# The last 256 tokens of a final RMSNorm transposed on TensorE before they are scaled, and the output stored in fewer, larger pieces

## The chip, the core and the metric

One Trainium2 chip, of which the kernel uses one core. The time is that of the device, in microseconds (us) from the launch to the end, for one execution; a median of several executions is given. The core has five engines with a queue each, worked in order: TensorE (PE, matmuls; PEld is its loading of the stationary operand), VectorE (DVE), ScalarE (ACT), GpSimd (POOL) and SyncE (SP, which here only issues DMA transfers). ACT and POOL can issue transfers too. Matmuls write to PSUM; the other tiles lie in SBUF. Both have 128 partitions.

## The reference

One layer of a hybrid mixer over 1024 tokens of 1024 features, in float32, and a final RMSNorm:

```python
shift, scale, gate = jnp.split(c_act @ mod_w[l] + mod_b[l], 3, axis=-1)
h = rmsnorm(x, norm_g[l]) * (1.0 + scale[:, None, :]) + shift[:, None, :]
cv, cg, cs, lx, ls = jnp.split(h @ w_in[l], [...], axis=-1)
v = causal_depthwise_conv(cv * jax.nn.sigmoid(cg), dw_w[l], dw_b[l])
v = jax.nn.silu(layernorm(v, cln_g[l], cln_b[l])) @ pw2_w[l] + pw2_b[l]
y_conv = v * jax.nn.silu(cs)
...
y_lru = linear_scan(a, mult * (i * xs)) * jax.nn.silu(ls)
y = jnp.concatenate([y_conv, y_lru], axis=-1) @ w_out[l]
x = x + (1.0 + gate[:, None, :]) * y
return rmsnorm(x, final_g)
```

The change touches the last three lines: `x` is what the kernel calls `fin`, and `rmsnorm` divides each token by the root of its mean square over the features and multiplies each feature by `final_g`.

## The kernel before

**Layout.** Everything is kept turned: features on partitions, tokens along the free axis. A tile `fin{m}` holds features 128m to 128m+127 of all 1024 tokens. A mean over features is therefore a sum over partitions and over eight tiles. The output leaves in the same layout, one row of the DRAM tensor a feature, and the host transposes it.

**Products.** A float32 product is three matmuls in a faster format: each operand is split into a high and a low part (`wh`, `wl`, `bh`, `bl` in `pair_products` and `tail_mm`), and low times low is left out. For pairs of output tiles, `pair_products` (L593) forms seven block products for eight: "1", "z", "2", "3", "4", "y" and "s", in the order of a string. "1", "2", "3" and "4" add up in one PSUM buffer `x` and in between ACT copies it to SBUF (`fout` after "1", `eout` after "2" and "3"): the next product into `x` has to wait for that copy. `OUT7` holds the strings for the product with w_out, for its three pairs; tile 6 comes before them and tile 7 (`OUT_Z`) is formed as a plain product.

**The scheduler.** `S` is a `Plan`, a list scheduler that runs when the program is built. Each operation has an engine, an estimated cost and a priority (the first argument, lower is earlier), reads and writes. Plan simulates the engines with these costs and so fixes the order of each engine's queue. The constants near the top (`ZP`, `NPZ`, `APART`, `SQP0`, `QGATES`, ...) are priorities and gates by which that order was adjusted; the order is no longer changed on the chip.

**The end.** The output is finished in three stretches of tokens, `END = ((0, 512), (512, 768), (768, 1024))`. `last_tiles` forms tile 7 of a stretch with 24 matmuls (L658; `out` in the profile). `gated` multiplies by 1 + gate and adds x (DVE, L360). `squares` squares each tile on ACT and sums the squares: tile 6 begins the sum `finss`, the others are added to it by DVE, and tile 7's are kept apart in `finsqz`, so that they need not be added.

`norm(n, a, e)` then makes the final norm of a stretch, through `rstd`: PE multiplies `finss` and `finsqz` by a column of ones (L680), which leaves the sum of squares of 128 tokens as one column of PSUM; ACT takes the root (`sd`), DVE the reciprocal (`rs`, L695). Since tokens lie along the free axis of `fin`, one more pair of matmuls spreads it: `rs` broadcast as the stationary operand times the identity (`spread`, L686) gives a PSUM tile `finbc` that holds 1/rms of every token on all partitions:

```python
pe.matmul(ps()[:, o + b * P:o + b * P + P],
          rs()[:, b:b + 1].to_broadcast([P, P]), ident, start=True, stop=True)
```

For the last stretch PE spreads it twice, into `finbc` for DVE and into `idle` for ACT, and executes seven matmuls without use (`warm_mm`, L676) in between. DVE makes `o = fin * final_g * finbc` for five or six of the eight tiles (L360), and POOL the others (L368), from a copy `bc` that ACT makes of the spread (L341) and from tiles `fin` that ACT has multiplied by `final_g`. Each of the eight tiles of a stretch is stored by itself (`store`, L392): eight stores of 256 KB for the first 512 tokens (2 KB rows), eight of 128 KB for each of the other stretches (1 KB rows); SP issues 18 of them and ACT six.

## Time and profile before

| | |
|---|---|
| time, median of 3 executions | 736.63 us (736.36 to 737.24) |
| time of the profiled execution | 736.94 us |
| its span, from the first instruction to the last | 735.2 us |
| granted TensorE clock | 0.999 |
| instructions | 8918 |

The profile is of one execution. Its span is 1.7 us shorter than that execution's time, which has the launch and the end around it. A row of a timeline gives the start, the length, the engine, the line of the kernel, the operation, its output and inputs (buffer numbers left out), their shapes as partitions x elements, the number of instructions and, in brackets, how long the engine was idle before and what ended that. PEq, DVEq, ACTq and SPq are the engines' sequencers, which issue transfers and wait for semaphores. In the table of windows each engine has its busy time and its number of instructions. An fp32 matmul leaves two records and a matmul in the faster format one.

### The profile page before, as it was taken

The page shows a single profiled execution, that of the slowest core. Times are in us where ns is not written, and L with a number is a line of the kernel's source. Part 1 is how long each engine was busy: PE and PEld are TensorE (multiplying, and loading weights), DVE is VectorE, ACT ScalarE, POOL GpSimd, SP SyncE. Part 2 cuts the span into 40 slices and gives each one's busy share as a digit, 9 for nine tenths or more (in the row PEclk, how much of TensorE's full clock was granted, in tenths as well). Part 3 has the DMA queues.
Part 4 walks back from the last instruction along what each step waited for, and adds up shares of the span by engine and source line. Part 5 has one row for each costly group of instructions (what it writes and reads, how often), then busy time and mean ns, then how long its engine had stood idle before and what let it go on. Part 6 is the DMA issues. An engine that isn't in the chain of part 4 may idle for free.

```text
span 735.2 us, 8918 instructions
## 1 busy us (share of the span) xinstructions
PE 727.7 (99%) x3312; PEld 605.8 (82%) x3312; DVE 623.7 (85%) x844; ACT 448.0 (61%) x563; POOL 110.0 (15%) x113
## 2 busy tenths in 40 slices
PE   9999999999999999999999999999999999999996
PEld 8888888888888888888888888878888888888886
DVE  7999999889979996887698999658799667999745
ACT  7650688556699968857859777334754323665432
POOL 0022001222312332321201110620000000000003
PEclk9999999999999999999999999999999999999999
DMA  9960045696979999789644453425233530522306
GB/s 341 407 221 29 0 131 120 142 211 149 237 177 227 211 211 225 160 178 213 129 113 100 114 104 109 163 97 201 86 114 111 177 114 1 204 94 103 115 1 229
DMA packets 37484, 111.59 MB, mean 152 GB/s; under 512 B 4160, under 2 KB 12864, under 8 KB 37440
## 3 DMA queue, kind: packets, MB, share of 16 engines
q1 hardware_dynamic: 24048, 75.97, 29.0%
q0 software_dynamic: 12528, 34.26, 26.3%
q10 hardware_dynamic: 864, 0.79, 0.3%
q8 instruction: 26, 0.43, 0.2%
q14 instruction: 18, 0.15, 0.1%
HBM read 64.16 MB, written 12.58 MB: 104 GB/s over the span
## 4 chain that ended last, share of the span: by engine, by line
PE 98%; DVE 1%; ACT 0%; DVEq 0%; issue 0%
PE ps L485 65%; PE xpw L607 6%; PE first L761 5%; PE xout L607 4%; PE ypw L607 3%; PE gate L1167 3%; PE out L658 2%; PE yout L607 2%; PE zpw L607 1%; PE zout L607 1%; DVE o L360 1%; PE late L761 1%; PE token_stats L718 1%; PE c_row L722 0%; PE token_stats L890 0%; PE vout L607 0%
## 5 line engine op out<-in xcount | busy, mean ns | idle before, releaser
L485 PE MATMUL ps<-ul,whi 128*128 128x512 f32 x576 | 177.4, 389 | 0.0
L485 PE MATMUL ps<-uh,whi 128*128 128x512 f32 x576 | 177.4, 389 | 0.0
L485 PE MATMUL ps<-uh,wlo 128*128 128x512 f32 x576 | 177.3, 389 | 0.0
L485 PEld LDWEIGHTS ps<-ul,whi 128*128 128x128 f32 x576 | 108.1, 188 | 22.5
L485 PEld LDWEIGHTS ps<-uh,wlo 128*128 128x128 f32 x576 | 108.1, 188 | 22.5
L485 PEld LDWEIGHTS ps<-uh,whi 128*128 128x128 f32 x576 | 108.1, 188 | 22.3
L341 ACT CAST whi<-raw 128x1024 fp32r<-128x1024 f32 x46 | 48.2, 1050 | 65.6 <-PE ps L485 52.4
L373 POOL DMA_DIRECT2D es<-cq x45 | 39.2, 872 | 230.1 <-ACT cq L349 209.7
L368 DVE TENSOR_TENSOR wlo<-raw,whi 128x1024 fp32r<-128x1024 f32 x42 | 52.3, 1244 | 14.0 <-ACT whi L341 14.0
L349 ACT ACT_TABLE_LOAD x45 | 57.7, 1283 | 1.5 <-PEq L1476 0.7
L360 DVE SCALAR_TENSOR_TENSOR cacc<-v,V,cacc 128x511 f32<-128x511 f32 (+14 forms) x75 | 55.8, 744 | 0.5
L360 DVE SCALAR_TENSOR_TENSOR caccs<-c,wsum,caccs 128x511 f32<-128x511 f32 (+6 forms) x70 | 52.1, 745 | 0.9
L360 DVE SCALAR_TENSOR_TENSOR caccs<-v,V,caccs 128x511 f32<-128x511 f32 (+6 forms) x70 | 52.1, 744 | 0.9
L373 POOL DMA_DIRECT2D oo<-co x42 | 40.4, 974 | 58.2 <-ACT co L349 21.1
L368 POOL TENSOR_TENSOR o<-fin,bc 128x256 f32<-128x256 f32 (+1 forms) x7 | 6.1, 892 | 242.2 <-ACT bc L341 242.2
L485 PE MATMUL ps<-yh,whi 128*128 128x512 f32 x128 | 40.0, 394 | 0.0
L485 PE MATMUL ps<-yl,whi 128*128 128x512 f32 x128 | 39.5, 389 | 0.0
L485 PE MATMUL ps<-yh,wlo 128*128 128x512 f32 x128 | 39.4, 389 | 0.0
L360 DVE SCALAR_TENSOR_TENSOR xs<-ps,V,xs 128x1023 f32<-128x1023 f32 (+2 forms) x24 | 30.6, 1276 | 2.9 <-ACT xs L349 2.9
L349 ACT ACTIVATE cq<-v,V 128x511 f32<-128x511 f32 (+14 forms) x45 | 31.8, 706 | 0.1
L349 ACT ACTIVATE cq<-c,wsum 128x512 f32<-128x512 f32 x42 | 29.7, 711 | 0.0
L349 ACT ACTIVATE co<-v,V 128x511 f32<-128x511 f32 (+13 forms) x42 | 29.2, 707 | 0.6 <-DMA oo<-co 0.6
(333 smaller groups left out, 1423.7 us busy)
## 6 DMA issues: line engine op xcount, KB each, us to landing
raw<-in_w_in_dram SPq DMA_DIRECT2D x36, 512.0 KB, 4.6
modw<-in_mod_w_dram SPq DMA_DIRECT2D x24, 512.0 KB, 8.7
raw<-in_w_out_dram SPq DMA_DIRECT2D x10, 512.0 KB, 3.9
scsd<-scs SPq DMA_DIRECT2D x8, 512.0 KB, 3.6
accd<-acc SPq DMA_DIRECT2D x8, 512.0 KB, 2.8
rawpw<-in_pw_dram SPq DMA_DIRECT2D x8, 512.0 KB, 3.5
scsr<-scsd SPq DMA_DIRECT2D x8, 512.0 KB, 5.4
fin<-accd SPq DMA_DIRECT2D x8, 512.0 KB, 4.6
```

The source lines that it names most:

```text
L341: act.copy(out(), in_())
L349: act.activation(out=out(), in_=in_(), func=func, **kw)
L360: dve.scalar_tensor_tensor(out=out(), in0=in0(), scalar=scalar, in1=in1(), op0=op0, op1=op1, accum_out=accum)
L368: lambda: e.tensor_tensor(out=out(), in0=a(), in1=b(), op=op), prio, r, w,
L373: return S.op("POOL", ISSUE, lambda: pool.dma_start(out(), a(), accum_op=ALU.add), prio, r, w, lag=RATE * n / T, after=after)
L485: pe.matmul(ps()[:, a - off:b - off], k3(lhs)()[:, k, :], rhs[k]()[:, a:b], start=(k == 0 and lhs is wh and rhs is xh and (a - off) % H == 0),
L607: pe.matmul(half(ps, 0)(), half(*lhs)()[:, j * P:j * P + P], half(*rhs)(), start=start and j == 0 and t == 0, stop=j == KT // 2 - 1 and t ...
L658: pe.matmul(ps()[:, a - off:e - off], k3(lhs)()[:, k, :], rhs()[:, i * H + a % H:i * H + a % H + e - a], start=k == KORD[0] and lhs is wh ...
L718: pe.matmul(psb()[:, :P], ones, ones, start=True, stop=True)
L761: pe.matmul(ps()[:, a - off:b - off], fw_part(lhs, k, i * P, i * P + P)(), rhs()[:, a:b], start=k == 0 and lhs is wh and rhs is xh, stop=k ...
L1167: pe.matmul(ps()[:, c0:c1], lhs()[:, j, :], rhs()[:, c0:c1], start=st == 0, stop=st == 2)
```

## The change

The stretches 0 to 511 and 512 to 767 keep their norm, but their tiles `o` are grouped by the table `STORES`: two tiles to a store for the first, which makes four stores of 512 KB, and one or two for the second, five stores. A store's rows lie one after the other in DRAM, in the layout of the tile, and the host puts them in place.

The last 256 tokens are turned over. ACT (for tile 7, DVE) multiplies `fin` by `final_g` into two tiles `turn0` and `turn1`, four features' tiles in each. The new function `turned` transposes them, 128 features by 128 tokens at a time, with 16 matmuls that have the data as the stationary operand and the identity as the moving one, into a PSUM tile for each 128 tokens (`turned768_0`, `turned768_1`), tokens on partitions and 1024 features along the free axis. There 1/rms is one number a partition: `rs` is used as it is, without a spread, in four scalings of 512 features, two on DVE (L1428) and two on ACT (L1425). Four stores of 256 KB follow, issued by SP. The second spread, the matmuls without use, the copy `bc`, POOL's products and the stores from ACT's queue are gone from this stretch. The buffer of the spread for tokens 512 to 767 comes from another pool. The square root's table is loaded by a square root of no use (`junk`), which a product of the last pair but one releases, instead of at the first norm. Gates, priorities and one order string differ.

```diff
@@ -46,29 +46,33 @@
...
-QGATES = ((2, 5), (3, 1), (3, 4), (3, 1))
+QGATES = ((2, 5), (3, 3), (3, 4), (3, 1))
 OUT_A, OUT_P, OUT_Z = (6,), (0, 1, 2), (7,)
 KORD = (0, 1, 2, 3, 4, 5, 6, 7)
-ZP = (0, 0.5)
-NPZ = (0, 1.5)
-APART = (0, 2.35, 0.8)
-Z0P = 1
+ZP = (-0.5, 1)
+NPZ = (-1, 1.5)
+APART = (0, 2, 0.5)
+Z0P = 0.6
 NP0 = 0.3
-SQP0 = 0.6
-SQP1 = 3.0
+SQP0 = 0.9
+SQP1 = 2.5
 ORDER7 = "1z2y3s4"
 PW7 = (("1z2y3s4",), ("1y2z3s4",), ("1y2z3s4",), ("1y2z3s4",))
-OUT7 = (("1zsy234",), ("1z2y34", "s"), ("z1234", "ys"))
+OUT7 = (("1z2sy34",), ("1z2y34", "s"), ("z1234", "ys"))
...
-AP = {0: (), 512: (1, 5), 768: (1, 3, 5, 7)}
-NP = {0: (6, 0), 512: (6, 0, 7), 768: (6, 0)}
+STORES = {0: ((2, 3), (6, 4), (5, 7), (1, 0)), H: ((1,), (2, 6), (3, 0), (4, 5), (7,))}
+NP = {0: (6, 0, 1), H: (6, 0, 7)}
+TURN = 1.7
+TURNA = 1
+TURNV = 1
+TURNO = ("DVE", "ACT")
+WHOLE = (False, False)
...
-WARM = (5, 2)
...
@@ -390,7 +394,7 @@
...
-                    moved=n * P * 4 / 340e3)
+                    moved=n * P * 4 / 380e3)
...
@@ -664,16 +668,12 @@
...
-    def rstd(prio, sqs, a, e, ps, o, after=(), warm=(), idle=None):
+    def rstd(prio, sqs, a, e, ps, o, after=()):
...
-
-
-        def warm_mm():
-            pe.matmul(half(idle, 0)()[:, :P], ones, ones, start=True, stop=True)
...
@@ -686,17 +686,12 @@
...
-            at = S.op("PE", 0.18 * nb, lambda sq=sq, k=k: stats(sq, k), prio, halves(sq, a, e), wk,
+            S.op("PE", 0.18 * nb, lambda sq=sq, k=k: stats(sq, k), prio, halves(sq, a, e), wk,
                       after=after if k == 0 else [])
-            for _ in range(warm[k] if warm else 0):
-                S.op("PE", 0.22, warm_mm, prio, [], [idle], after=[at], columns=4 * P)
...
-        if idle:
-            S.op("PE", 0.22 * nb, lambda: spread(idle), prio, [rs], [idle], after=[op],
-                 columns=4 * P * nb)
...
@@ -1351,32 +1346,94 @@
...
-                tail_mm(n, ps, a, ("out", m), y_sets, k, a, e)
+                o = tail_mm(n, ps, a, ("out", m), y_sets, k, a, e)
             firm.append(gated(n, m, ps, a, e, a))
             squares(m, n, a, e, qz)
+        return o
...
-        bc = mm_tile(f"finbc{a}") if a == H else acc_tile(f"finbc{a}")
-        b2 = mm_tile("idle") if e == T else bc
-        rstd(n, [ss, qz], a, e, bc, 0, warm=WARM if e == T else (), idle=b2 if e == T else None)
+        bc = acc_tile(f"finbc{a}")
+        rstd(n, [ss, qz], a, e, bc, 0)
...
-        ACT(n + 0.2, part(bs, 0, w_), part(b2, 0, w_), "copy", w_, r=[b2], w=[bs])
+        ACT(n + 0.2, part(bs, 0, w_), part(bc, 0, w_), "copy", w_, r=[bc], w=[bs])
+        to, at = {}, a
+        for g, ms in enumerate(STORES[a]):
+            o = big_buf(f"o{a}_{g}", parts=4)
+            to.update({m: (o, i * w_, i * w_ + w_) for i, m in enumerate(ms)})
         for m in (*NP[a], *(i for i in range(KT) if i not in NP[a])):
-            o, t = big_buf(f"o{a}_{m}"), acc[m]
+            t, (o, x, y) = acc[m], to[m]
             if m in NP[a]:
-                TT(D0 + 20, "POOL", part(o, 0, w_), part(t, a, e), part(bs, 0, w_), ALU.mult, w_,
-                   r=halves(t, a, e) + [bs], w=[o])
+                TT(D0 + 20, "POOL", part(o, x, y), part(t, a, e), part(bs, 0, w_), ALU.mult, w_,
+                   r=halves(t, a, e) + [bs], w=halves(o, x, y))
             else:
-                STT(D0 + 20, part(o, 0, w_), part(t, a, e), vec("final_g", m), part(bc, 0, w_),
-                    ALU.mult, ALU.mult, w_, r=halves(t, a, e) + [bc], w=[o], after=firm[-1:])
-            store(D0 + 20, "ACT" if m in AP[a] else "SP",
-                  lambda m=m, a=a, e=e: out[m * P:(m + 1) * P, a:e], part(o, 0, w_), [o], w_)
+                STT(D0 + 20, part(o, x, y), part(t, a, e), vec("final_g", m), part(bc, 0, w_),
+                    ALU.mult, ALU.mult, w_, r=halves(t, a, e) + [bc], w=halves(o, x, y),
+                    after=firm[-1:])
+        for ms in STORES[a]:
+            o, w = to[ms[0]][0], len(ms) * w_
+            rows = out[at:at + P * w // T, :].rearrange("r (h f) -> (r h) f", f=w)
+            store(D0 + 20, "SP", lambda rows=rows: rows, part(o, 0, w), halves(o, 0, w), w)
+            at += P * w // T
+    def turned(n, at, a, e, before):
+        w_, nb = e - a, (e - a) // P
+        ps = [mm_tile(f"turned{a}_{b}") for b in range(nb)]
+        stat = acc_tile(f"finbc{a}")
+        sd, rs = S.buf("sd", f"sd{a}"), S.buf("rs", f"rs{a}")
+        order = [m for m in range(KT) if m not in OUT_Z] + list(OUT_Z)
+        def where(m):
+            x = m % 4 * w_
+            return part(turns[m // 4], x, x + w_), (turns[m // 4], m % 4)
+        def turn(m, b):
+            x = where(m)[0]()
+            pe.matmul(ps[b]()[:, m * P:m * P + P], x[:, b * P:b * P + P], ident, start=True,
+                      stop=True)
+        def sums(sq, k):
+            for b in range(nb):
+                pe.matmul(stat()[:, b:b + 1], sq()[:, a + b * P:a + b * P + P], ones[:, 0:1],
+                          start=k == 0 and b == 0, stop=k == 1, skip_group_check=True)
+        for m in OUT_Z:
+            x, key = where(m)
+            TS(n, x, part(acc[m], a, e), vec("final_g", m), None, ALU.mult, n=w_,
+               r=halves(acc[m], a, e), w=[key])
+        S.op("PE", 0.18 * nb, lambda: sums(ss, 0), n, halves(ss, a, e), [stat])
+        for ms in (order[:-len(OUT_Z)], OUT_Z):
+            for b in range(nb):
+                for m in ms:
+                    S.op("PE", 0.12, lambda m=m, b=b: turn(m, b), at, [where(m)[1]],
+                         [(ps[b], m * P // H)], columns=4 * P, after=[before])
+        S.op("PE", 0.18 * nb, lambda: sums(qz, 1), n, halves(qz, a, e), [stat])
+        ACT(n, lambda: sd()[:, :nb], lambda: stat()[:, :nb], AF.Sqrt, nb, bias=eps_t,
+            scale=1.0 / D, r=[stat], w=[sd])
+        S.op("DVE", 0.2, lambda: dve.reciprocal(rs()[:, :nb], sd()[:, :nb]), n, [sd], [rs])
+        for b in range(nb):
+            o = big_buf(f"o{a}_{b}", parts=2)
+            def scaled(z, b=b, o=o):
+                if TURNO[b] == "ACT":
+                    act.activation(out=half(o, z)(), in_=half(ps[b], z)(), func=AF.Copy,
+                                   scale=rs()[:, b:b + 1])
+                else:
+                    dve.tensor_scalar(out=half(o, z)(), in0=half(ps[b], z)(),
+                                      scalar1=rs()[:, b:b + 1], scalar2=None, op0=ALU.mult)
+            for z in (0, 1):
+                S.op(TURNO[b], 0.62, lambda z=z, f=scaled: f(z), n, [rs, (ps[b], z)], [(o, z)])
+            r = a + b * P
+            for z in (range(0, 2),) if WHOLE[b] else (range(0, 1), range(1, 2)):
+                x, y = z[0] * H, z[-1] * H + H
+                store(D0 + 20, "SP", lambda r=r, x=x, y=y: out[r:r + P, x:y], part(o, x, y),
+                      [(o, i) for i in z], y - x)
...
@@ -1398,6 +1455,7 @@
...
+            ACT(n, lambda: junk, lambda: eps_t, AF.Sqrt, 1, w=[("junk", 0)], after=last[1:])
...
@@ -1418,11 +1476,18 @@
...
+    turns = [big_buf(f"turn{j}", parts=4) for j in range(KT // 4)]
+    for m in range(KT):
+        if m not in OUT_Z:
+            b, x, w = turns[m // 4], m % 4 * (T - END[-1][0]), T - END[-1][0]
+            ACT(n - TURNV, part(b, x, x + w), part(acc[m], T - w, T), AF.Copy, w,
+                scale=vec("final_g", m), r=halves(acc[m], T - w, T), w=halves(b, x, x + w),
+                after=last[TURNA:TURNA + 1])
     for i, (a, e) in enumerate(END[1:]):
-        last_tiles(n + ZP[i], a, e)
-        if i:
-            norm(n + NPZ[0], *END[i])
-    norm(n + NPZ[1], *END[-1])
+        product = last_tiles(n + ZP[i], a, e)
+        if i == 0:
+            norm(n + NPZ[i], a, e)
+    turned(n + NPZ[i], n + TURN, a, e, product)
...
@@ -1480,4 +1545,14 @@
...
-    return np.ascontiguousarray(r.results[0]["out_0_dram"].T)[None]
+    y, o = r.results[0]["out_0_dram"], np.empty((T, D), np.float32)
+    at = 0
+    for a, groups in STORES.items():
+        w = dict(END)[a] - a
+        for ms in groups:
+            n = P * w * len(ms) // T
+            o[a:a + w].reshape(w, KT, P)[:, ms] = \
+                y[at:at + n].reshape(P, len(ms), w).transpose(2, 1, 0)
+            at += n
+    o[at:] = y[at:]
+    return o[None]
```

With the tables and priorities the order of the queues moves. On PE, the end of the program before, from the last matmul of tile 7 on (`out` is that product, `rs_0` the 1/rms of tokens 512 to 767, `rs64.5_0` that of the last 256):

```order
L658 MATMUL out_768_5615<-yhb_5020,wlo_5431 128x256
L686 MATMUL finbc_5639<-ident,rs_0_5656 128x128 x2
L680 MATMUL finbc_5664<-ones,finss 128x1 x2
L676 MATMUL idle<-ones 128x128 x5
L680 MATMUL finbc_5664<-ones,finsqz 128x1 x2
L676 MATMUL idle<-ones 128x128 x2
L686 MATMUL finbc_5664<-ident,rs64.5_0_5702 128x128 x2
L686 MATMUL idle<-ident,rs64.5_0_5702 128x128 x2
```

and after the change, where the spread of `rs_0` stands six matmuls ahead of the last one, and the turns (L1399) behind it:

```order
L662 MATMUL out_768_5619<-yhb_5018,wlo_5428 128x256
L1404 MATMUL finbc_5671<-ones,finss 128x1 x2
L1399 MATMUL turned_0_5676<-ident,turn_5492 128x128 x4
L1399 MATMUL turned_0_5676<-ident,turn_5503 128x128 x3
L1399 MATMUL turned_1_5690<-ident,turn_5492 128x128
L1404 MATMUL finbc_5671<-ones,finsqz 128x1 x2
L1399 MATMUL turned_1_5690<-ident,turn_5492 128x128 x3
L1399 MATMUL turned_1_5690<-ident,turn_5503 128x128 x3
L1399 MATMUL turned_0_5676<-ident,turn_5503 128x128
L1399 MATMUL turned_1_5690<-ident,turn_5503 128x128
```

The block that follows the last product has no wait for 1/rms in it any more; the turn of tile 7 comes last for both tiles.

On DVE, the end after the change, with the semaphores that each row waits for (`o_2` and `o_3` are tiles of tokens 512 to 767):

```order
L364 SCALAR_TENSOR_TENSOR o_2_5680<-fin_5162,V,finbc_5629 128x256
L386 TENSOR_SCALAR turn_5503<-fin_5347,V 128x256 [waits DVE_49]
L364 SCALAR_TENSOR_TENSOR o_3_5694<-fin_5330,V,finbc_5629 128x256
L364 SCALAR_TENSOR_TENSOR o_3_5694<-fin_5340,V,finbc_5629 128x256
L1419 RECIPROCAL rs_5707<-sd_5702 128x2 [waits Activation_49]
L1428 TENSOR_SCALAR o_0_5713<-turned_0_5676,rs_5707 128x512 [waits DVE_49,PE_49]
L1428 TENSOR_SCALAR o_0_5713<-turned_0_5676,rs_5707 128x512
```

Only the first of the two scalings waits for PE.

On ACT, the place where the table load went, in the last pair of tiles but one, before:

```order
L341 COPY eout_5319<-xout_5208 128x512
L349 ACTIVATE fin_5030<-fin_5030,V 128x512
L349 ACTIVATE fin_5030<-fin_5030,V 128x256 x2
L349 ACTIVATE finsq_0_5340<-fin_5149 128x512
L341 COPY fout_5234<-yout_5315 128x512
L341 CAST hlout_5356<-rawout_1_5278 128x512
L341 COPY eout_5319<-xout_5208 128x512
```

and after:

```order
L345 COPY eout_5318<-xout_5203 128x512
L353 ACTIVATE fin_5029<-fin_5029,V 128x512
L353 ACTIVATE fin_5029<-fin_5029,V 128x256
L353 ACT_TABLE_LOAD
L353 ACTIVATE junk<-eps_t 128x1
L345 COPY fout_5232<-yout_5314 128x512
L345 CAST hlout_5349<-rawout_1_5280 128x512
L353 ACTIVATE finsq_0_5358<-fin_5158 128x512
L345 COPY eout_5318<-xout_5203 128x512
```

The second `eout` copy now has the squares `finsq` ahead of it, and the table load stands ahead of `fout`.

## The prediction

> **What bounds the kernel now.** I read the page first, for the busy times and the shares of the chain of waits, to see whether one engine sets the whole time or the stages differ.
>
> ```profile
> PE 727.7 (99%) x3312; PEld 605.8 (82%) x3312; DVE 623.7 (85%) x844; ACT 448.0 (61%) x563; POOL 110.0 (15%) x113
> ...
> PE 98%; DVE 1%; ACT 0%; DVEq 0%; issue 0%
> ```
>
> TensorE (PE) is 98% of the chain, so everything up to its last product is worth only what PE waits or executes. The change removes none of the split products. It can pay in two places: PE's waits ahead of the last product, and the tail behind it. How long the tail is, the windows of the last 15 us show (columns: stretch, length, busy time and count of PE, weight load, DVE, ACT, POOL, clock, DMA share, GB/s).
>
> ```profile
> 720.00:725.00 5.00, 4.92 (x42) 4.72 (x41) 4.16 (x9) 1.82 (x4) 0.72 (x1) 1.00 0.99 367
> 725.00:730.00 5.00, 3.84 (x33) 3.46 (x31) 3.83 (x11) 1.32 (x4) 2.62 (x4) 1.00 0.66 221
> 730.00:735.20 5.20, 0.00 (x0) 0.00 (x0) 1.03 (x3) 0.00 (x0) 0.90 (x2) 0.80 0.69 226
> ```
>
> PE is full to 725, and in the last 5.2 us it does nothing: there DVE, the stores' transfer and the completion remain. The chain of waits, in order of time, says what leads from the last product to the last scaling (start, length, what).
>
> ```profile
> 724.78 0.46 PE finbc L686 x4
> ...
> 725.67 2.05 DVE o L360 x5
> 727.71 0.09 DVE rs64.5_0_5702 L695
> ...
> 727.84 0.72 PE finbc L686 x4
> ```
>
> The last products (out, L658) end at about 724.6; the norm of the last 256 tokens cannot end before DVE has done five scalings of the tokens before them, then the reciprocal, PE's spread of 1/rms (L686) and DVE's six scalings, which start at 728.59. PE's own rows around it give the pitches I need (start, length, what; an fp32 matmul leaves two records).
>
> ```profile
> 724.50 0.28 PE L658 MATMUL out<-yhb,wlo 128*128 128x256 f32 x1
> 724.62 0.60 PE L686 MATMUL finbc<-ident,rs 128*128 128x128 f32 x4
> 725.06 0.51 PE L680 MATMUL finbc<-ones,finss 128*128 128x1 f32 x4
> 725.43 1.36 PE L676 MATMUL idle<-ones 128*128 128x128 f32 x10
> 726.62 0.50 PE L680 MATMUL finbc<-ones,finsqz 128*128 128x1 f32 x4
> ```
>
> From start to start: a spread of two blocks 725.06 - 724.62 = 0.44 us; two statistics matmuls 0.37; five matmuls of 128x128, 726.62 - 725.43 = 1.19, so 0.24 each (0.22 in the spread). What follows the last scaling is the transfer (rate in slices of 0.25 us from 726.00; then SP's store instructions, first and last issue).
>
> ```profile
> GB/s 33 25 25 25 238 344 336 217 348 176 340 353 324 352 324 348 336 348 328 356 332 332 357 328 344 344 336 348 336 262 4 0 0 0 0 0 0 0 0 0
> ```
> ```profile
> L392 SPq DMA_DIRECT2D out_dram<-o x18: 332/393/413, 718.9 to 731.2; - x18
> ```
>
> The last store is issued at 731.2, the data ends at 733.5 (slice 30), and the span of 735.2 ends 1.7 us behind the data. From 728 on the transfer runs without a gap at some 340 GB/s: the end is bound by the rate of the stores at least as much as by DVE.
>
> **The change part by part.** All of it is summed against the profiled execution, span 735.2 and time 736.94, which lies 0.31 above the median of 736.63.
>
> *Ahead of the last product.* The arithmetic on PE is the same; six yout products (1.36 us) merely stand earlier. What can change is waiting. Two waits of PE's weight loads stand where the order changes (total, times, longest); below them are ACT's rows and the chain's at the pair of output tiles around 682.
>
> ```profile
> PEld yout L607 <- DVE yla L368: 0.3, 1, 0.3
> PEld xout L607 <- ACT eout L341: 0.5, 2, 0.3
> ```
> ```profile
> 682.15 0.64 ACT L349 ACTIVATE finsq<-fin 128x512 f32<-128x512 f32 x1 [0.49 <-PE yout L607]
> 682.70 0.56 ACT L341 COPY fout<-yout 128x512 f32<-128x512 f32 x1
> 684.33 0.62 ACT L341 CAST hlout<-rawout 128x512 fp32r<-128x512 f32 x1 [1.07 <-DVE finss L368]
> 685.10 0.59 ACT L341 COPY eout<-xout 128x512 f32<-128x512 f32 x1
> ...
> 713.90 1.28 ACT L349 ACT_TABLE_LOAD   x1
> 715.20 0.26 ACT L349 ACTIVATE sd61.3_0_5549<-finbc,eps_t 128x4 f32<-128x4 f32 x1
> ```
> ```profile
> 685.07 1.36 PE zout L607 x6
> 686.42 2.72 PE xout L607 x12
> ```
>
> The waits for yla and for one eout go with the later gate and the new order of the last pair's products: a gain of at most 0.3 + 0.3, and I take 0.4. Against it, the copy eout, which frees the buffer that PE's xout products at 686.42 write again, moves behind finsq (0.64) on ACT, and the table load for the square root (1.28) moves from 713.90 to a place ahead of fout. The load falls into ACT's idle time (1.07 ahead of 684.33), and hlout still waits for DVE until 684.33. Then hlout 0.62, finsq 0.64 and eout 0.59 end at about 686.2 instead of 685.7. PE, by then 0.4 early, wants the buffer at 686.4 - 0.4 - 0.2 of weight load = 685.8: a wait of about 0.4. The two cancel: **0**, with ends of -0.6 (all waits gone, none new) and +0.6. At 713.90 the load was followed by sd only, and PE's spread behind it is covered by products; its absence there gains nothing.
>
> The row at 715.20 starts 0.02 us behind the load's end. By "ScalarE: Activation LUTs" in the Trainium skill, section "What ACT_TABLE_LOAD costs", each switch also pays a drain of about 1.38 us; an estimate by that page would put 1.38 - 1.07 = 0.3 us more on PE's wait and the total 0.3 higher. The row shows no such drain, so I go by the row.
>
> *PE's last stretch.* The spread for tokens 512 to 767 (0.44) now stands ahead of the last six products, so the last product ends 0.44 later: 724.62 + 0.44 = 725.06 (up to 0.3 later still, if the reciprocal isn't there, since its statistics stand nine products ahead of it and the chain between them takes some 0.9 against 9 x 0.12 = 1.1 us; 0.12 is the step of a 256-wide product, 724.62 - 724.50). Removed are seven warm-up matmuls and the second spread, which lay in PE's wait for 1/rms. Added are 16 turns of 128x128, at 0.23 each from the two pitches above. The first DVE scaling waits for the whole tile of the first 128 tokens, whose last turn is the 15th: 15 x 0.23 + 2 x 0.37 = 4.2 us behind 725.06. With the 0.31 that DVE needed behind the old spread's end (727.84 + 0.44 = 728.28, scaling at 728.59) it starts at **729.6**; ACT's tile is one turn later, 729.8. 1/rms does not bind: the finsqz statistics end at 725.06 + 0.37 + 8 x 0.23 + 0.37 = 727.6, and square root and reciprocal took 727.84 - 726.99 = 0.85 before, so it is there at 728.5. So the last 1/rms no longer sits in the chain, but 4.2 us of PE do, where before 728.59 - 724.62 = 4.0 us passed to the same point; with the 0.44 and the longer latency **1.0 is lost** up to the first scaling (729.6 against 728.6).
>
> *Scalings and stores.* Group rows give what a 512-wide operation takes (busy, mean ns); the row below them is DVE's last block, the scalings that the change replaces.
>
> ```profile
> L360 DVE SCALAR_TENSOR_TENSOR o<-fin,V,finbc 128x512 f32<-128x512 f32 x6 | 4.2, 742 | 1.3 <-ACT bc L341 1.3
> ...
> L341 ACT COPY bc<-finbc 128x512 f32<-128x512 f32 x1 | 0.6, 588 | 1.4 <-PE finbc L686 1.4
> ```
> ```profile
> 728.59 2.44 DVE L360 SCALAR_TENSOR_TENSOR o<-fin,V,finbc 128x256 f32<-128x256 f32 x6 [0.81 <-PE finbc L686]
> ```
>
> Before: six scalings of 256 on DVE, 2.44 us, beside two on POOL. Now two of 512 on DVE and two on ACT side by side. A scaling with one tensor from PSUM and a number per partition is not in the trace; it lies between the copy (0.59) and the two-tensor form (0.74), and I take 0.65, nearer the copy. So the four stores are ready at 730.25, 730.45, 730.9 and 731.1, against a last issue at 731.2 before: the scaling is 1.1 us shorter and **gives that 1.0 back**. The seven ACT scalings and one DVE scaling into the tiles to be turned lie earlier, beside PE's products (ACT has 39% idle); the seventh tile's, on DVE, is done by 726.7, well ahead of its turn.
>
> What is left is the transfer. The stores of tokens 0 to 511 show what rows of 2 KB reach (slices of 0.525 us from 715.00), and the first of them the first issue.
>
> ```profile
> GB/s 0 0 0 0 0 0 0 0 0 359 386 386 382 378 379 382 339 312 367 297 12 23 35 328 283 267 338 340 341 336 343 343 341 336 341 47 0 0 0 0
> ```
> ```profile
> 718.90 12.70 SPq L392 DMA_DIRECT2D out_dram<-o  x18
> ```
>
> Some 380 GB/s at 2 KB, against 340 at 1 KB. The first issue is at 718.90; the tenth slice, from 719.73, is the first with data, so data starts some 0.8 behind an issue. The four last stores hold 4 x 262 KB = 1.05 MB, or 2.76 us at 380. First issue 730.3, data from 731.1 to 733.9, end at 733.9 + 1.7 = **735.6, 0.4 later than before**. The stores of tokens 512 to 767 are out of the way by then: their last scaling is done by some 728 (it is 727.7 in the chain now), and 1.05 MB from 727.5 takes until 730.3. At 340 GB/s it would be 0.3 more; were the rate no bound, the last issue (SP's steps of 0.39, so 731.5) plus 0.8, 0.35 for a store at twice the rate and 1.7 gives 734.4, 0.8 less than before. Fewer stores free SP's queue, which did not bind: 18 issues of 0.39 us are spread over 12.7 us.
>
> In "DMA: Bandwidth & Descriptors" of the Trainium skill, section "Specifications", 16 engines of 27 GiB/s make 464 GB/s; by that, an estimate, the four stores would take 2.26 us and the end come 0.5 us sooner, so that the tail would be even. The trace shows 380, and I go by it.
>
> **Sum:** 0 (waits ahead) + 0.4 (tail) = +0.4 on the profiled 736.94, so 736.63 + 0.4 = **737.0** for the median: no change. About 0.2%, 1.5 us, is what a measurement of this kernel can tell from none.
>
> **The rivals.** *The transfer is no bound and the waits ahead vanish* (faster): -0.8 in the tail and -0.6 ahead give 735.2. For it: the rate above the last stores' own need was never seen, and ACT has much idle time. Against it: 340 GB/s without a gap in the last 5 us, and eout's place behind finsq.
>
> *First halves before the last turn* (a little faster): if the first 512 columns of each turned tile wait only for their own turns and 1/rms (728.5), the first store goes out at 729.2 instead of 730.3; data from 730.0 to 732.8 gives -0.7, or 735.9. Against it: in the order the second scaling has no wait of its own, so the first carries the wait for the whole tile. "PSUM — Partial Sum Buffer" in the Trainium skill, section on bank collisions, says to guard by bank, by which the halves, a bank each, could be taken apart; no run here shows it yet.
>
> *ACT's queue holds PE* (slower): in the last pair five of the scalings into the turned tiles stand on ACT ahead of the copy eout that frees PE's buffer. They wait for a PE product first. A group of three such operations shows their price.
>
> ```profile
> 680.15 1.52 ACT L349 ACTIVATE fin<-fin,V 128x512 f32<-128x512 f32 x3
> ...
> 704.21 0.59 ACT L341 COPY eout<-xout 128x512 f32<-128x512 f32 x1 [1.64 <-PE xout L607]
> ```
> ```profile
> 704.17 1.36 PE out L658 x6
> ```
>
> Five at about 0.45 are 2.3 us. Where they begin 1.6 ahead of 704.2, the copy is 0.7 late and the 1.36 us of six out products behind which PE needs the buffer hide it; where they begin only at 704.2, it is 2.3 late and PE waits about 1.5. It decides from a release later than about 703.5. With the tail's 0.4 that makes 738.5. For it: they stand in front of it in an in-order queue. Against: 1.64 us idle ahead of eout, and the tiles they read are long done.
>
> **How the numbers follow.** Forecast (even) 0.62, rate no bound 0.15, first halves 0.07, ACT holds PE 0.16. The forecast's own spread about 737.0 is -0.9 (waits -0.6, and 0.3 less up to the first scaling) to +0.9 (+0.6 and the slower rate's 0.3). Eight in ten reach from 735.2 to 738.5, which are the ends of the first and the last rival. Faster by over 0.2% (below 735.16): half of the no-bound case, and 0.1 for a PE stretch that is also shorter than its pitches say, 0.18; slower (above 738.1): most of the ACT case and a little of the forecast, 0.17; the same 0.65.
>
> **What would show it.** In the changed profile: PE's last product at about 725.1; the turns as a block of 4.2 us without waits; the first DVE scaling at 729.6, 0.6 to 0.7 long; four issues from 730.3; data at about 380 GB/s from 731.1 to 733.9; a wait of PE for eout of some 0.4 us near 686, and none of over 0.5 near 705. Wrong would be: turns at another pitch than 0.23 (0.05 each is 0.8 us), first scaling ahead of the last turn, a gap in the transfer, or a PE wait above 1 us ahead of 720.

## The result: 0.2% slower, and the profile after

Over 19 executions each, the changed kernel takes 738.12 us (median; 737.52 to 740.48), the one before 736.92 (736.22 to 737.49): ratio 1.0022, 95% interval 1.0015 to 1.0029. The forecast was 737.0 and no change. (A ratio, here and below, is to the kernel before, executed beside the other.) The profiled execution took 738.09 with a span of 736.2, 1.0 more than before.

The windows of the end, with the columns as before:

```profile
720.00:725.00 5.00, 3.97 (x34) 3.77 (x33) 3.86 (x6) 1.19 (x3) 3.12 (x3) 1.00 0.62 248
725.00:730.00 5.00, 5.00 (x46) 5.00 (x46) 3.24 (x8) 1.05 (x3) 2.10 (x3) 1.00 0.85 317
730.00:736.20 6.20, 0.29 (x3) 0.10 (x1) 1.41 (x2) 1.26 (x2) 0.00 (x0) 0.75 0.60 223
```

The turns are there: from 725 to 730 PE is full where it was busy for 3.84 us. But between 720 and 725, where it was full before (4.92), it lacks a whole microsecond, and that lies ahead of the turns. The chain of waits says what it waited for:

```profile
719.52 0.74 DVE o L364
720.26 1.73 DVE finss L372
721.99 0.04 issue
722.03 0.61 PE finbc L680 x4
...
725.11 0.71 PE out L662 x6
725.82 0.34 PE finbc L1404 x4
726.16 1.89 PE turned L1399 x16
728.05 0.34 PE finbc L1404 x4
728.39 1.91 PE turned L1399 x16
730.30 0.02 issue
730.33 0.69 ACT o L1425
```

From 719.52 to 721.99 the chain is now on DVE: an addition to `finss`, the sum of squares over the tiles, is the last thing that the statistics of tokens 512 to 767 need. Before, it took 0.68 us, POOL was through with its multiplications by then (718.17 + 2.55 = 720.72), and PE's statistics followed without an idle time in brackets.

```profile
718.17 2.55 POOL L368 TENSOR_TENSOR o<-fin,bc 128x512 f32<-128x512 f32 x2 [235.52 <-ACT bc L341]
721.82 0.68 DVE L368 TENSOR_TENSOR finss<-finss,finsq 128x512 f32<-128x512 f32 x1
722.55 0.61 PE L680 MATMUL finbc<-ones,finss 128*128 128x1 f32 x4
```

After, it is 1.80 us long, PE's statistics have an idle time of 1.03 us in brackets, and POOL multiplies beside it.

```profile
718.90 4.22 POOL L372 TENSOR_TENSOR o<-fin,bc 128x512 f32<-128x512 f32 x3 [236.25 <-ACT bc L345]
720.18 1.80 DVE L372 TENSOR_TENSOR finss<-finss,finsq 128x512 f32<-128x512 f32 x1
722.03 0.61 PE L680 MATMUL finbc<-ones,finss 128*128 128x1 f32 x4 [1.03 <-DVE finss L372]
730.10 1.41 DVE L1428 TENSOR_SCALAR o<-turned,rs 128x512 f32<-128x512 f32 x2 [1.21 <-PE turned L1399]
```

The transfer of the end, in slices of 0.25 us from 727.00: it stops at 730.9, starts again at 731.7 and runs at some 380 GB/s to 734.5.

```profile
GB/s 246 352 58 16 16 205 377 410 369 393 340 348 385 393 381 115 29 25 74 369 385 361 410 393 336 393 393 369 393 328 8 0 0 0 0 0 0 0 0 0
```

To compare profiles I use three distances, all from PE's timeline and the span: F, the start of the first product of w_in (it lies at 7.5 to 8.7 from one execution to the next, whatever the kernel); L, the start of the instruction behind the last product of tile 7; and the end of the span. L - F holds everything ahead of the tail.

| kernel | F | L - F | last addition to finss | end - L | median of executions |
|---|---|---|---|---|---|
| before | 8.15 | 716.47 | 0.68 | 10.54 | 736.92 |
| changed | 8.14 | 717.52 | 1.80 | 10.55 | 738.12 |

The tail is the same to 0.01 us. All of the loss, 1.05 us, lies ahead of the last product. Of it the forecast had 0.44: the spread of tokens 512 to 767, which lies behind L in the kernel before (and in e2, e6 and e10 below) and ahead of L in the changed one.

### The profile page after: what moved, and what is told of

Its sections match the earlier page's. It is cut to its first block, busy times and chain, and to the rows that moved or that the text cites. A ratio compares the mean times of both kernels' runs of the same rounds, so it can differ in the third digit from the quotient of the medians.

```text
span 736.2 us, 8914 instructions
## 1 busy us (share of the span) xinstructions
PE 728.2 (99%) x3322; PEld 606.7 (82%) x3322; DVE 623.8 (85%) x840; ACT 450.8 (61%) x571; POOL 110.1 (15%) x112
## 4 chain that ended last, share of the span: by engine, by line
PE 98%; DVE 0%; ACT 0%; issue 0%; ACTq 0%
PE ps L489 65%; PE xpw L611 6%; PE first L756 5%; PE xout L611 4%; PE ypw L611 3%; PE gate L1162 3%; PE out L662 3%; PE yout L611 2%; PE zpw L611 1%; PE zout L611 1%; PE late L756 1%; PE token_stats L713 1%; PE turned L1399 1%; PE token_stats L885 0%; PE c_row L717 0%; PE vout L611 0%
## 5 line engine op out<-in xcount | busy, mean ns | idle before, releaser
L372 POOL TENSOR_TENSOR o<-fin,bc 128x512 f32<-128x512 f32 (+1 forms) x6 | 6.3, 1082 | 238.7 <-ACT bc L345 238.7
```

The lines of the kernel that those rows point to most:

```text
L372: lambda: e.tensor_tensor(out=out(), in0=a(), in1=b(), op=op), prio, r, w,
```

## The experiments

The theory (A): DVE's addition has two operands in SBUF, POOL's multiplication too, and the one that starts second is held until the other is done. Rivals: the tail costs (T), or the stores' transfer holds the addition (D). And for the five executions at 739.9 to 740.5: PE's pause sometimes costs granted clock (C). The experiments stand in four sets, e1 to e4, e5 to e8, e9 to e12 and e13 to e16, each set on a chip of its own.

**e1: the addition's new operand in PSUM.**

```diff
-            q = big_buf(f"finsq{m}_{a}")
+            q = mm_tile(f"finsq{m}_{a}", 1) if (m, a) == (4, H) else big_buf(f"finsq{m}_{a}")
...
-               r=[*sk, q], w=sk)
+               r=[*sk, q], w=sk).lock = True
```

The second edit keeps the scheduler's own account of the addition, and with it the order, as it was.

> The changed kernel, with the order of every engine's instructions unchanged; only the squares that DVE adds to finss last (tile 4, tokens 512 to 1023) are written to PSUM instead of SBUF, so that this one addition has an operand outside SBUF. Theory A (DVE's addition of two SBUF tensors is held while POOL multiplies two SBUF tensors, the statistics wait for it, and PE with them): the addition takes about 0.7 us instead of 1.80 though POOL's work beside it is the same, PE's wait for finss falls from 1.03 to about 0.2, the last product ends 0.9 earlier and the time falls by 0.9, from 738.1 to 737.2. Rival T (the tail of turns and stores is what costs, the long addition only fills time that is lost anyway): the time stays at 738.1. Rival D (the stores' transfer, not POOL, holds the addition): the addition stays at about 1.8 us.

Measured: 736.75 beside 736.74 before, ratio 1.0002 (0.9993 to 1.0010). In its timeline POOL works as before and the addition falls into the midst of it:

```profile
718.77 3.77 POOL L372 TENSOR_TENSOR o<-fin,bc 128x512 f32<-128x512 f32 x3 [236.26 <-ACT bc L345]
720.05 0.68 DVE L372 TENSOR_TENSOR finss<-finss,finsq 128x512 f32<-128x512 f32 x1
720.78 0.61 PE L680 MATMUL finbc<-ones,finss 128*128 128x1 f32 x4
```

0.68 us, no wait in brackets, and POOL's three scalings also take 0.45 less. T and D fall: the same tail, and the same stores beside it.

**e2: the kernel before, with POOL kept busy.**

```diff
-                TT(D0 + 20, "POOL", part(o, 0, w_), ...
+                x = TT(D0 + 20, "POOL", part(o, 0, w_), ...
+                if a == 0 and m == NP[0][-1]:
+                    def again(once=x.emit, o=o, t=t, bs=bs):
+                        once()
+                        pool.tensor_tensor(out=o()[:, :H // 2], in0=t()[:, :H // 2],
+                                           in1=bs()[:, :H // 2], op=ALU.mult)
+                        once()
+                    x.emit = again
```

> The kernel before, with the order unchanged; POOL repeats its second scaling of the first stretch (once at half width, once whole), so that it is still busy when DVE makes its last addition to finss at 721.8 us. Theory A: that addition takes about 1.5 us instead of 0.68, PE's wait for finss grows from 0.3 to about 1.1, and the time by 0.8, from 736.9 to 737.7. Rivals T and D: nothing changes but POOL's busy time; 736.9.

Measured: 738.12 beside 736.74, ratio 1.0019 (1.0010 to 1.0028). The kernel before gets the whole loss of the change from two operations on an engine that was off the path:

```profile
721.76 1.28 POOL L368 TENSOR_TENSOR o<-fin,bc 128x512 f32<-128x512 f32 x1
721.96 1.64 DVE L368 TENSOR_TENSOR finss<-finss,finsq 128x512 f32<-128x512 f32 x1
723.65 0.60 PE L680 MATMUL finbc<-ones,finss 128*128 128x1 f32 x4 [1.03 <-DVE finss L368]
```

POOL's scaling ends at 723.04, and 723.04 + 0.56 is the addition's end: it does nothing until POOL is through. In the order of the kernel before, then, the hold alone makes the loss. L - F rose by 0.96 and the median by 1.4, where 0.8 were expected.

**e3: PE's pause filled.**

```diff
+        def filled():
+            for _ in range(6):
+                pe.matmul(ps()[:, o + P:o + 2 * P], ones, ones, start=True, stop=True)
+            stats(sqs[0], 0)
...
```

> The changed kernel, with six matmuls of no use (128x128, about 1.3 us) on PE ahead of the statistics of tokens 512 to 767, that is, in PE's wait for finss. The addition stays at 1.8 us and the wait of 1.2 us is filled; the typical time is 738.1 to 738.3. Theory C (the executions at 739.9 to 740.5, 5 of 19, are those in which PE's pause of 1 us costs granted clock): no execution over 739.5. Rival (they come from the transfers or elsewhere): about a quarter stays near 740.

Measured: 737.51 (737.16 to 738.42, 11 executions), ratio 1.0010 (1.0001 to 1.0019); none near 740. The addition is still held (1.82 us). L - F is 717.51, as in the changed kernel, so the useless matmuls cost nothing; why the median is 0.6 below the changed kernel's, which was not executed beside it, was not seen in the profile.

**e4: the turned tiles cut by features instead of tokens.**

```diff
-            pe.matmul(ps[b]()[:, m * P:m * P + P], x[:, b * P:b * P + P], ident, ...)
+            pe.matmul(half(ps[m // 4], b)()[:, m % 4 * P:m % 4 * P + P], x[...], ident, ...)
...
-        for ms in (order[:-len(OUT_Z)], OUT_Z):
+        for ms in ((0, 1, 2, 3), (4, 5, 6), (7,)):
...
```

> The changed kernel with the turned tiles cut the other way: one PSUM tile holds features 0 to 511 of both blocks of 128 tokens, the other features 512 to 1023, and the stores go in that order. The first scalings then wait for eight turns and 1/rms, not for 15 turns. If the tail is bound by the first scaling and the transfer behind it: first scaling at 729.0 instead of 730.1, first of the four stores issued at 729.8 instead of 730.9, the span 1.0 shorter, 737.1. If the transfer of the stores of tokens 512 to 767 (data until 730.7) is in the way: 0.2 to 0.3 shorter, 737.8. PE's wait for finss is unchanged in both.

Measured: 737.50, ratio 1.0013 (1.0004 to 1.0022). DVE's first scaling comes much earlier, 3.34 us behind L instead of 4.44, but the end follows by 0.30 only (end - L 10.25). The rate row of its transfer, from 727.00, and the windows of its end (the last two columns are DMA share and GB/s) show why:

```profile
728.36 0.75 DVE L1429 TENSOR_SCALAR o<-turned,rs 128x512 f32<-128x512 f32 x1
729.69 0.75 DVE L1429 TENSOR_SCALAR o<-turned,rs 128x512 f32<-128x512 f32 x1 [0.57 <-PE turned L1399]
```
```profile
GB/s 16 0 90 393 385 369 389 373 336 365 397 377 393 344 393 385 377 393 377 393 393 385 385 238 25 33 8 0 0 0 0 0 0 0 0 0 0 0 0 0
```

```profile
732.00:732.75 0.75, 0.00 (x0) 0.00 (x0) 0.00 (x0) 0.00 (x0) 0.00 (x0) 1.00 1.03 388
732.75:733.00 0.25, 0.00 (x0) 0.00 (x0) 0.00 (x0) 0.00 (x0) 0.00 (x0) 1.00 0.65 238
733.00:733.65 0.65, 0.00 (x0) 0.00 (x0) 0.00 (x0) 0.00 (x0) 0.00 (x0) 1.00 0.07 25
```

The gap at 731 is gone: the stores of tokens 512 to 767 and the last four now run into one another. The transfer at full rate ends at 732.9, which is 7.9 behind L against 8.8 in the changed kernel, so 0.9 of the 1.1 arrived. But then some 0.75 us follow at 25 GB/s and a DMA share of 0.07, that is, about one of the 16 engines still at work; they take back most of it. Why one engine ends later is not shown. The 0.3 is what the second of the two expectations had, but not for its reason.

**e5: e1 and e4 together.**

> The changed kernel with both edits that helped alone: the last squares for finss in PSUM, and the turned tiles cut by features. Seen against the last product, the tail of the cut by features alone was 0.26 us shorter, and its transfer ran without a gap from 727.75 on. Theory A with the transfer as the tail's bound: the addition takes 0.7, no wait of PE, and the time is 738.1 - 1.0 - 0.3 = 736.8 to 736.4, at or just below the kernel before. Rival (the tail follows the first scaling, which comes 1.1 earlier): 735.7.

Measured: 736.67 beside 736.86, ratio 0.9996 (0.9987 to 1.0005); addition 0.68, end - L 10.26, with the same 0.75 us of one engine at the end. The two add up as expected, and that is no faster than the kernel before.

**e6: PE's statistics back behind 15 products.**

```diff
                 o = tail_mm(n, ps, a, ("out", m), y_sets, k, a, e)
+                if a == END[-1][0] and k == KORD[4]:
+                    for x in begun:
+                        S.hold(x, o)
...
```

> The changed kernel with PE's statistics of tokens 512 to 767 back behind 15 of the 24 products of the last tile (as in the kernel before) instead of behind 6; the spread follows the last product then. Theory A: DVE's addition is still held to 1.8 us, but 9 products of 0.12 more cover it: PE's wait falls from 1.03 to about 0.1. The spread's 0.44 moves behind the last product, so the gain is 0.9 or less: 737.2. Rival (the position is all that matters and the length of the addition nothing): the addition is 0.7 long here. Rival T (tail): 738.1.

Measured: 737.30, ratio 1.0005 (0.9996 to 1.0014). The time is about as expected, but not for the reason given: in the profile, which is of the lowest of the 11 executions (736.31), the addition is 0.68 long, with POOL at work. In the records POOL's second scaling begins at 719.819 and DVE's addition at 719.832; DVE went first, and POOL's scaling took 1.85. In the changed kernel's profile the two are 23 ns apart, and POOL went first. So the position was not tested in this execution, and a new question stood there: who wins.

**e7: the turning alone undone.**

```diff
-STORES = {0: (...), H: (...)}
+STORES = {0: (...), H: (...), 768: ((1,), (2, 6), (3, 0), (4, 5), (7,))}
-NP = {0: (6, 0, 1), H: (6, 0, 7)}
+NP = {0: (6, 0, 1), H: (6, 0, 7), 768: (6, 0)}
...
-    turned(n + NPZ[i], n + TURN, a, e, product)
+    norm(n + NPZ[i], a, e)
```

> The changed kernel with the turning alone undone: the last 256 tokens go through the spread and the scalings of 256 as before, but without matmuls of no use, with one spread, and in grouped stores; everything else as changed. DVE's last addition to finss stands ahead of POOL's work in this order, so no hold is expected. If the turned tail is about as long as the old one (10.54 and 10.55 us from the last product to the end in the two profiles): 736.9 less the spread that now stands ahead (0.44) and the faster rate of larger rows, 736.2 to 736.5. If turning is worth something by itself: over 737.0, that is, slower than the first experiment's 736.75.

Measured: 736.67 (735.38 to 737.73), ratio 0.9996 (0.9987 to 1.0004). In its profile end - L is 9.95, 0.60 less than with turning, and L - F 716.21. PE pauses twice behind the last product, as its waits say:

```profile
PE finbc L681 <- ACT finsqz L354: 1.1, 1, 1.1
PE finbc L687 <- DVE rs64.5_0_5684 L694: 0.6, 1, 0.6
```

**e8: the changed kernel again.**

> The changed kernel once more, unchanged, for its executions near 740 (5 of 19 so far). Theory C (a pause of PE of 1 us sometimes costs granted clock): about 3 of 11 near 740, and none in the experiments without a pause; if the profile catches one, its granted clock is about half for some 4 us behind 721 and full elsewhere. Rival (the clock is lost at the start of the program, or it is no matter of the clock): the same 3 of 11, with the loss elsewhere in the profile, or none at all.

Measured: 737.76, 2 of 11 executions at 739.86 and 739.87; the profile has a usual one (738.09, addition 1.80).

**e9: POOL meets the addition with a short operation.**

```diff
-                TT(D0 + 20, "POOL", part(o, x, y), ...
+                op = TT(D0 + 20, "POOL", part(o, x, y), ...
+                if a == 0 and m == NP[0][0]:
+                    def again(once=op.emit, o=o, t=t, bs=bs, x=x):
+                        once()
+                        pool.tensor_tensor(out=o()[:, x:x + 128], in0=t()[:, :128],
+                                           in1=bs()[:, :128], op=ALU.mult)
+                    op.emit = again
```

> The changed kernel, with the order unchanged; POOL repeats 128 columns of its first scaling before it begins the second, so that DVE's last addition to finss meets this short operation (about 0.4 us) and not the beginning of a scaling of 1.28 us. Theory A in its sharper form (the addition is held for the rest of the one POOL instruction under way, then goes first): the addition takes about 1.0 us instead of 1.80, although POOL has more to do; PE's wait falls from 1.18 to about 0.4, the time by 0.75, from 738.0 to 737.2. Rival (it is held as long as POOL has work, or both share the access and slow each other): 1.8 or longer, 738.0 or more.

Measured: 736.59 beside 737.03, ratio 0.9996 (0.9988 to 1.0005). More work for POOL, and L - F is 1.16 us less than in the changed kernel's profile:

```profile
720.11 0.91 POOL L1377 TENSOR_TENSOR o<-fin,bc 128x128 f32<-128x128 f32 x1
```
```profile
720.02 0.68 DVE L372 TENSOR_TENSOR finss<-finss,finsq 128x512 f32<-128x512 f32 x1
```

The short operation waits for the one before it and so begins 0.09 behind the addition: now DVE is first and is not held at all (1.0 was expected), and it is POOL's 128 columns that take 0.91. So the rest of a POOL instruction under way, which the expectation put at 0.4, was not met at all. Whether the addition waits for one instruction or for all of POOL's work, the changed kernel's profile says: POOL's third scaling is lengthened in its turn (1.73 instead of 1.28), so the addition went ahead of it.

```profile
721.39 1.73 POOL L372 TENSOR_TENSOR o<-fin,bc 128x512 f32<-128x512 f32 x1
```

**e10: e6 with DVE surely second.**

```diff
+                def later(once=op.emit):
+                    for _ in range(2):
+                        dve.tensor_scalar(out=macc[:, 0:1], in0=macc[:, 0:1], scalar1=1.0, ...)
+                    once()
...
```

The edit of e6 stands in it too.

> The kernel with the statistics behind 15 products, and two DVE operations of one column each ahead of the addition (a factor of 1.0), so that POOL's second scaling surely begins first; without them DVE began within 13 ns of POOL in the profile and was not held. The addition takes 1.6 to 1.8 us; the nine products cover it, PE's wait is 0.1 to 0.3 instead of 1.03, and the time is 737.0 to 737.3. If the cover does not matter: 738.0.

Measured: 737.60, ratio 1.0007 (0.9998 to 1.0016). The addition takes 1.58. PE's weight loads wait 0.2 for `finss` and 0.3 for `finsqz`, whose chain on DVE stands behind the addition. L - F is 0.69 above e6's (both profiles are of the lowest of 11 executions): of the 0.90 of the hold and the 0.25 of the two operations ahead of it the nine products cover less than half.

**e11 and e12: the changed kernel, one execution each.**

> The changed kernel, one look more for an execution near 740 (7 of 30 so far) with a profile. Theory C: the granted clock is about half for some 4 us behind PE's pause at 721 to 722 and full elsewhere. Rival: the loss lies at the start, or the clock is full and the loss a wait. A time of 737.3 to 738.4 tells nothing on this.

> The changed kernel, a second look for an execution near 740 with a profile. Theory C (a pause of PE of 1 us sometimes costs granted clock): about half the clock for some 4 us behind 721. Rival: the loss is elsewhere. A usual time tells nothing on this.

Measured: 736.47 and 736.38, lower than any of its 30 executions until then. The same program, with the other winner:

```profile
718.41 4.35 POOL L372 TENSOR_TENSOR o<-fin,bc 128x512 f32<-128x512 f32 x3 [236.22 <-ACT bc L345]
```
```profile
719.69 0.68 DVE L372 TENSOR_TENSOR finss<-finss,finsq 128x512 f32<-128x512 f32 x1
```

POOL's second scaling began 13 ns ahead of the addition in the records; the addition is not held, POOL's scaling takes 1.83, and PE does not wait.

**e13, e14, e15: more of the changed kernel.**

> The changed kernel, unchanged, in further executions. If the time hangs on which of DVE and POOL begins first, by some 10 to 30 ns (two looks with DVE first, 736.4; two profiles with POOL first, 738.1), the executions fall into groups: near 736.4 or 737 where DVE is first, 737.3 to 738.4 where POOL is, and some near 740. If a whole set of executions has one winner (30 of 30 had POOL so far, by their times), the median is one of the two and not between. Rival (the two looks were low for another reason, such as the start of the program): a median near 738.0 whatever the profile shows of the addition.

> The changed kernel, one more look at which engine is first and for an execution near 740 with a profile. DVE first: addition 0.68 us, 736.1 to 737.2. POOL first: 1.80 us, 737.3 to 738.4, or near 740 with about half the granted clock for some 4 us behind PE's pause, if the pause is what costs it.

> The changed kernel, a last look of the same kind. DVE first: addition 0.68 us, 736.1 to 737.2. POOL first: 1.80 us, 737.3 to 738.4, or near 740 with about half the granted clock for some 4 us behind PE's pause.

Measured: e13 has 737.52 as its median, but its 12 executions are six from 736.27 to 737.25, four from 737.80 to 738.37 and two at 739.88 and 740.03. Its profile is one of the low ones (736.40, addition 0.68, 14 ns). So the winner changes within one set of executions. e14 and e15 caught two near 740 (739.99 and 740.16), both with POOL first (28 and 15 ns) and the addition 1.80 and 1.81. The windows of e14, the first of which holds the pause:

```profile
720.50:722.50 2.00, 0.97 (x9) 0.77 (x8) 2.00 (x3) 0.00 (x0) 2.00 (x3) 1.00 0.82 330
722.50:723.80 1.30, 1.30 (x12) 1.30 (x12) 1.30 (x3) 0.93 (x2) 1.04 (x1) 1.00 0.76 299
723.80:727.20 3.40, 3.40 (x18) 3.40 (x19) 0.50 (x3) 0.64 (x2) 0.00 (x0) 0.52 0.68 266
727.20:730.00 2.80, 2.80 (x27) 2.80 (x26) 2.80 (x7) 0.42 (x1) 2.11 (x3) 0.97 0.63 226
```

The column behind POOL's is the granted clock: 1.3 us behind the pause it falls to half for 3.4 us, while PE is full, and comes back. Products of 256 columns step by 0.21 us there (724.18, 724.39, 724.61) instead of 0.12. e15 has the same, 0.55 from 723.9 to 727.4.

**e16: the old tail with its useless matmuls.**

```diff
-        rstd(n, [ss, qz], a, e, bc, 0)
+        rstd(n, [ss, qz], a, e, bc, 0, (), (5, 3) if e == T else (),
+             mm_tile("idle") if e == T else None)
```

> The kernel with the turning undone and the stores grouped, with eight matmuls of no use back in PE's two waits behind the last product (1.1 and 0.6 us there). Its profile without them was 0.85 us shorter than that of the kernel before, counted from PE's first product of w_in, but its executions spread from 735.4 to 737.7. If PE's pauses cost clock in some of them: a narrower spread and a median of 736.0 to 736.3, below both kernels. If the spread has another cause: 736.7 again.

Measured: 736.14 (735.56 to 736.87) beside 736.91, ratio 0.9992 (0.9983 to 1.0000). It is the lowest of all and lies below both kernels, though against the one before its interval reaches to 1. The executions spread over 1.3 us instead of e7's 2.4; whether that is the clock was not seen in a profile.

The distances for all that decide something:

| kernel | F | L - F | last addition | end - L |
|---|---|---|---|---|
| e1, operand in PSUM | 8.01 | 716.40 | 0.68 | 10.55 |
| e2, before, POOL busy | 8.29 | 717.43 | 1.64 | 10.52 |
| e3, pause filled | 7.46 | 717.51 | 1.82 | 10.55 |
| e4, cut by features | 7.51 | 717.51 | 1.80 | 10.25 |
| e5, e1 and e4 | 8.34 | 716.34 | 0.68 | 10.26 |
| e6, statistics late, DVE first | 7.84 | 715.71 | 0.68 | 10.99 |
| e7, old tail | 7.96 | 716.21 | 0.69 | 9.95 |
| e9, short POOL operation | 8.02 | 716.36 | 0.68 | 10.55 |
| e10, statistics late, POOL first | 7.61 | 716.40 | 1.58 | 11.00 |
| e11, changed, DVE first | 7.69 | 716.36 | 0.68 | 10.57 |
| e14, changed, POOL first, half clock | 8.57 | 719.05 | 1.80 | 10.56 |
| e16, old tail, useless matmuls | 7.74 | 716.20 | 0.69 | 10.13 |

## Why the prediction was wrong

**The step that failed** is the one on PE's last stretch: "up to 0.3 later still, if the reciprocal isn't there, since its statistics stand nine products ahead of it". I bounded what comes behind the moved statistics and not what has to be there ahead of them. They moved from behind 15 products to behind 6, 9 x 0.12 = 1.1 us earlier, and their last input, DVE's addition to `finss`, has no term in the sum and so stood at its old 0.68. Unheld it is just in time: in e11 it starts at 719.69 and PE goes on without a wait. Held, it is 1.1 longer with no cover left, and PE waits 1.03. The hold is what costs: without it there is no loss (e1, e9), and with it the old order loses nearly as much (e2: 0.96). The earlier place of the statistics is the smaller part: back behind 15 products, less than half of the hold is covered (e6, e10). I had the rows of POOL in the profile and never laid them beside DVE's. The scheduler of both kernels even counts such a hold (`lock` and `held` in `Plan`); my sum did not. In the changed order the addition stands right behind two DVE scalings that the same copy `bc` releases as POOL's, and POOL is still at work then. Two scalings of 0.66 on DVE and one of 1.26 on POOL bring the addition and POOL's second scaling to within 30 ns of each other in every profile of the changed kernel.

The time lies inside the range that I gave, which went to 738.5. That is luck: this end stood for ACT holding PE, which did not happen. Of the signs of being wrong, a PE wait above 1 us, the one that came stands at 721 to 722 and not ahead of 720.

**Who is held is a race.** With 13 to 14 ns between the two starts DVE went first (e6, e11, e12, e13), with 15 to 29 ns POOL (the changed kernel's profile, e3, e4, e8, e14, e15). Of 46 executions of the changed kernel 8 lie from 736.27 to 737.25, 27 from 737.3 to 738.4 and 11 near 740. Seven of them have a profile: DVE was first in the three of the first group, POOL in the two of the second and the two near 740; of the other 39 the winner is inferred from the time. In the first group the change is worth about nothing: L - F 716.36 against 716.47, end - L 10.57 against 10.54. That is what I had forecast, but for the hold. "SBUF — State Buffer" in the Trainium skill, section "SBUF: two separate sides", says that DVE and GpSimd share a pair of ports under an exclusive lock, that an operation of DVE with two SBUF inputs takes part in it, and that whichever starts first has it for its whole instruction. The runs agree on the lock and on the whole instruction: with POOL first the addition ends 0.55 behind POOL's scaling (721.98 and 721.43 in the changed kernel's records), with DVE first POOL's scaling is 0.55 longer, and with one operand in PSUM neither is held (e1). On who starts first the records cannot decide: in e6, e11, e12 and e13 POOL's record begins first, by 13 to 14 ns, and DVE went first all the same.

**The other steps.** *Ahead of the last product* I took 0, a gain of 0.4 against a wait of 0.4 for `eout`. The gain came: the first product of the last tile starts at 720.13 on PE, where it started at 720.52 before. The wait did not: ACT's cast ahead of it was no longer waiting for DVE, and `eout` ended 0.7 earlier than I had it. *The table load* cost 1.28 and no drain, as the row had said: the small root behind it starts 0.01 later.

```profile
681.41 1.28 ACT L353 ACT_TABLE_LOAD   x1
682.70 0.20 ACT L353 ACTIVATE junk<-eps_t 128x1 f32<-128x1 f32 x1
682.81 0.57 ACT L345 COPY fout<-yout 128x512 f32<-128x512 f32 x1
683.28 0.62 ACT L345 CAST hlout<-rawout 128x512 fp32r<-128x512 f32 x1
684.38 0.63 ACT L353 ACTIVATE finsq<-fin 128x512 f32<-128x512 f32 x1 [0.49 <-DVE fin L364]
684.92 0.57 ACT L345 COPY eout<-xout 128x512 f32<-128x512 f32 x1
```

*The turns*: eight in 1.89 us, 0.236 each, against 0.23; the first DVE scaling 730.10 - 725.66 = 4.44 behind the last product against 4.5; a scaling 0.75 on DVE and 0.69 on ACT against 0.65; rate 380 against 380 (and not 464); end - L 10.55 against 735.6 - 725.06 = 10.54. The tail was right to 0.1 us in every term.

**The rivals.** *First halves before the last turn* did not happen, as the order had it, and in e4, which brings it about, the end gained 0.30 where the price was 0.7: the transfer at full rate ended 0.9 earlier, and one DMA engine's late end took most of that back. *ACT's queue holds PE* did not happen: `eout` of the last pair starts at 705.21, right behind the product, with no wait of PE. *The transfer is no bound* fell with the changed profile: the last four stores are issued from 730.9 to 732.3, and their data runs at 380 GB/s until 734.5. The forecast reached slower almost only through ACT; the mechanism that came true was not among the rivals.

**What the change gives by itself.** e7 against e1 sets the turned tail beside the old one with grouped stores: 10.55 against 9.95. In these two profiles turning costs 0.6 us of the tail; the medians, 736.75 and 736.67, do not show it. Without the hold, L - F is 0.11 below that of the kernel before although the spread's 0.44 now lies in it (e11), so some 0.55 us were gained ahead of the last product. What the grouped stores and the spread's new place give by themselves was not separated.

## What to carry to other kernels

When an operation is moved ahead, look at what has to be there before it, not only at what comes behind it; each microsecond of cover that goes lays bare the slowest of its inputs. An engine that is off the path can still hold one that is on it: lay the rows of POOL beside those of DVE and look for operations with all operands in SBUF that meet, above all where one event releases both. An operand in PSUM, or a few nanoseconds of order, takes the hold away, and a median that moves between sets of executions is a reason to look for such a race.

## What the hardware showed that I had not expected

A pause of PE of about 1.0 us was followed, in the two profiles that caught it, by 3.4 us at half the granted clock (0.52 in e14), 1.3 us behind the pause; it cost 719.05 - 717.51 = 1.5 us. Four other profiles with the same pause (the changed kernel's, e2, e4 and e8) kept the clock at 1.00. With the pause, 11 of the 38 executions of the changed kernel above 737.3 came near 740. None of 11 did with the pause filled (e3), and none of the 44 of e1, e5, e6 and e9, whose profiles have no such pause; but none of e2's 11 nor of e4's 11 did either, which pause for as long. So the pause fits as a cause and is not shown to be one, and what decides in which executions the clock falls stays open. "TensorE: Matmul & The Clock Gate" in the Trainium skill, section "Why this matters for your kernels", asks to avoid idle gaps over some 3 us; here half the clock followed a gap of a third of that, in two profiles of six.
